# Gate steps, merge loads and the final norm moved in a one-core encoder layer

## The chip, the cores and the metric

The kernel runs on one core of a Trainium2 chip. The metric is the device time of one execution in microseconds (us); the figure for a kernel is the median of its runs. TensorE (PE, with its weight loads PEld) multiplies; VectorE (DVE), ScalarE (ACT) and GpSimd (POOL) do the element-wise work; SyncE (SP) issues the transfers. Each engine runs its instructions in the order in which they are queued.

## The reference, cut to what matters

One layer of a streaming encoder works on 1024 prompt frames and 64 sample frames (T = 1088 columns) of width 1024, in float32.

```
h = x + 0.5 * SwiGLU_1(RMSNorm(x))
u = RMSNorm(h);  z = u @ W_in        -> q, k, v, q_idx, k_idx, w_idx, conv_in, gate
attn = top-k attention: per query the 256 best admissible keys by indexer score
       (48 for the sample frames), softmax over them, 8 heads on 2 key/value heads
conv = swish(LayerNorm(causal depthwise conv of GLU(conv_in))) @ conv_w_out
merged = sigmoid(g_a) * (attn @ attn_w_out) + sigmoid(g_c) * conv
h = h + merged @ W_out
h = h + 0.5 * SwiGLU_2(RMSNorm(h))
y = RMSNorm(h) * final_norm
```

The new keys, values, indexer keys and last convolution inputs are outputs too.

## The kernel before, in words

Activations lie transposed, channels on the 128 partitions and frames along the free axis. Every float32 product is made of three TensorE products (`mm3`, lines 134 to 138): weights and activations are split into a high part and a remainder, and high*high, high*low and low*high are added up in PSUM. So each operand is split first: ACT copies out the high part (L152 for activations, L118 and L326 for weights) and DVE or POOL subtracts (L153, L119, L327). The two SwiGLU stages use a 7-product scheme on 2x2 blocks of weights and halves of 272 frames (`wops`, `up`, `down`).

The stages follow each other: load x and take the sums of squares (`stats`, with `colsum` on TensorE, a Newton iteration on DVE in `rsqrt`, and `spread`, which puts the result on all partitions through TensorE and `ident`); SwiGLU 1 for two pairs of halves; the projections of u; indexer and top-k selection, while TensorE makes the first 12 of the 16 gate matrices (`GPRE`); attention; W_out; SwiGLU 2; final norm. Before the first SwiGLU, `prep` makes the split operands of the scheme out of the first half (POOL does half of the remainders) and then out of the second half.

**The attention stage** (L1172 to L1471) handles nine tiles of 128 queries (the last has 64) in the order 7, 6, 8, 5, 4, 3, 2, 1, 0, four pairs of heads each: 36 units. `soft` makes the logits in PSUM banks of the pool `lg` (3 banks; L1209, L1210), DVE adds the bias and takes the maximum (L1212), ACT takes the exponential and scales. `turn` transposes the shares on TensorE (`pt`, L1233) and splits them; `values` multiplies with the values (`pv`, one bank; L1253, L1254), and `oh` is stored to `d_at` (L1260, L1261). After each of the 84 slots `fill` (L1453) advances other work by a rate out of `RATE`, so that TensorE has something to do beside the softmax: `gate_part` (the last gate matrices, three steps of 24 products each, and the LayerNorm of chunk 2), `conv_part` (the convolution's output product for the three chunks of `CHUNKS`, with the other two LayerNorms; it reads gates `gc` and stores `d_mp`), `merge_part` (chunk 2: attention output product, both gates, split), `wout_part` (chunk 2 of W_out, added to h in DRAM) and `last_part` (merge of chunk 1). `merge` for a chunk may only begin when all tiles of the chunk are done (`ready`); its first step loads four pieces `ar` of `d_at` and splits them into `ah` and `al`. What is left, and chunk 1 and 0 of W_out, runs behind the attention.

The order on each engine is not the order of the program text: the tile framework schedules the instructions by priority (`high_priority`) and by its own estimate of when operands are there. Tiles of a pool are handed out in rotation, and a new tile waits until the old one in its place has been read.

**The end**: `tail_d` runs the sums of squares of the last two halves behind the last down products; `final` spreads the result and makes eight scalings on DVE (`scaled`, L211) of h by gain and by the spread row, each stored to y.

## Time and profile before

| | us |
|---|---|
| three runs | 2315.79, 2320.89, 2318.33 |
| median | 2318.33 |
| the profiled execution | 2322.28 |
| its span, first to last instruction | 2320.5 |
| TensorE busy in the span | 2244.1 |
| mean granted TensorE clock | 0.988 of full |

The span is 1.8 us shorter than the time of its execution. In the views below, a row of the timeline has start, duration, engine, line, operation, result and operands, shape, count, and in brackets the idle time of the engine ahead of it with what ended it. A row of waits has the sum, the number of times and the longest. A row of the chain has start, duration and what.

### The profile page before, as it was taken

To read this page: it belongs to the slowest core of one execution; us is meant where nothing else is said; L and a number is where in the kernel's file an instruction comes from. 1 tells how busy PE (TensorE), PEld (TensorE's weight loads), DVE (VectorE), ACT (ScalarE), POOL (GpSimd) and SP (SyncE) were. 2 spreads that over 40 slices of the span, in tenths; PEclk is the share of its full clock that TensorE was granted. 3 is DMA by queue.
4 is the path that set the end of the run, shared out by engine and by line. 5 is a ranking of instruction groups with operands and counts; after the bars stand their busy time and mean duration, and the time that the engine had idled before them with its cause. 6 is when DMAs were issued, how large, how long until landed. Compare 5 with 4: busy or idle time off the path is not lost. (4 is left out here: it accounts for less than half of the span.)

```text
span 2320.5 us, 44122 instructions
## 1 busy us (share of the span) xinstructions
PE 2244.1 (97%) x16226; PEld 2213.2 (95%) x16226; DVE 1672.9 (72%) x3816; ACT 1415.6 (61%) x2955; POOL 1440.0 (62%) x1003
## 2 busy tenths in 40 slices
PE   7999999999999999999989989899999999999997
PEld 6999999999999999999989989799999999999997
DVE  7887766777676378689956766567877667887765
ACT  7655555666546454797457877557665556555653
POOL 5677655677766593788711333367667666667754
PEclk9999999999999999999999999899999999999999
DMA  5322233233223434334422566652222332322323
GB/s 190 109 103 99 101 101 104 100 100 110 101 92 126 146 127 134 95 111 123 134 64 86 161 192 198 220 173 101 97 102 94 110 110 73 111 101 101 105 97 112
DMA packets 129547, 273.39 MB, mean 118 GB/s; under 512 B 17840, under 2 KB 77104, under 8 KB 129328
## 3 DMA queue, kind: packets, MB, share of 16 engines
q1 hardware_dynamic: 129328, 270.56, 35.1%
q8 instruction: 127, 2.08, 0.4%
q14 instruction: 92, 0.75, 0.1%
HBM read 231.82 MB, written 38.75 MB: 117 GB/s over the span
## 5 line engine op out<-in xcount | busy, mean ns | idle before, releaser
L136 PE MATMUL ps<-x,wp 128*128 128x272 f32 x1760 | 507.1, 289 | 6.2 <-ACT wp L152 3.3
L138 PE MATMUL ps<-x,wp 128*128 128x272 f32 x1760 | 503.7, 291 | 3.5 <-DVE wp L153 2.0
L137 PE MATMUL ps<-x,wp 128*128 128x272 f32 x1760 | 505.8, 288 | 0.0
L136 PE MATMUL ps<-x,whi 128*128 128x272 f32 (+2 forms) x1544 | 481.8, 312 | 6.4 <-ACT x L152 2.2
L153 POOL TENSOR_TENSOR wp<-s,wp 128x512 fp32r<-128x512 f32 x272 | 364.6, 1352 | 190.7 <-ACT wp L152 189.9
L138 PE MATMUL ps<-x,wlo 128*128 128x272 f32 (+2 forms) x1544 | 481.1, 312 | 0.0
L119 POOL TENSOR_TENSOR wlo<-raw,whi 128x1024 fp32r<-128x1024 f32 (+1 forms) x123 | 279.1, 2270 | 298.2 <-ACT whi L118 293.3
L137 PE MATMUL ps<-x,whi 128*128 128x272 f32 (+2 forms) x1334 | 412.1, 309 | 1.0 <-POOL x L153 1.0
L327 POOL TENSOR_TENSOR wlo<-raw,whi 128x1024 fp32r<-128x1024 f32 x120 | 290.1, 2418 | 179.5 <-ACT whi L326 161.5
L136 PEld LDWEIGHTS ps<-x,wp 128*128 128x128 f32 x1760 | 330.7, 188 | 9.9 <-ACT wp L152 4.8
L138 PEld LDWEIGHTS ps<-x,wp 128*128 128x128 f32 x1760 | 328.0, 188 | 6.9 <-DVE wp L153 3.8
L137 PEld LDWEIGHTS ps<-x,wp 128*128 128x128 f32 x1760 | 331.3, 188 | 0.0
L136 PEld LDWEIGHTS ps<-x,whi 128*128 128x128 f32 x1544 | 292.8, 190 | 8.7 <-ACT x L152 2.6
L138 PEld LDWEIGHTS ps<-x,wlo 128*128 128x128 f32 x1544 | 292.7, 190 | 1.0
L137 PEld LDWEIGHTS ps<-x,whi 128*128 128x128 f32 x1334 | 253.5, 190 | 2.5 <-POOL x L153 1.3
L152 ACT ACTIVATE wp<-s 128x512 fp32r<-128x512 f32 x272 | 167.9, 626 | 130.9 <-DVE s L314 83.6
L784 POOL TENSOR_TENSOR ac<-ac,pd 128x559 f32<-128x559 f32 (+1 forms) x132 | 194.8, 1476 | 23.0 <-ACT pd L783 15.5
L152 ACT ACTIVATE wp<-ps 128x512 fp32r<-128x512 f32 x208 | 123.1, 592 | 113.1 <-DVE ps L312 103.3
L439 DVE SCALAR_TENSOR_TENSOR h<-ps,h 128x272 f32<-128x272 f32 x448 | 175.0, 430 | 14.0 <-PE ps L138 12.7
L137 PE MATMUL ps<-gl,whi 128*128 128x272 f32 x640 | 183.4, 292 | 0.0
L137 PE MATMUL ps<-gl,wp 128*128 128x272 f32 x640 | 181.0, 288 | 0.0
L136 PE MATMUL ps<-gh,wp 128*128 128x272 f32 x640 | 179.0, 290 | 1.9 <-DVE h L439 1.8
(288 smaller groups left out, 5784.4 us busy)
## 6 DMA issues: line engine op xcount, KB each, us to landing
raw<-wf SPq DMA_DIRECT2D x353, 512.0 KB, 3.3
d_g<-sg SPq DMA_DIRECT2D x32, 181.0 KB, 1.9
d_h<-h SPq DMA_DIRECT2D x2, 2176.0 KB, 10.0
y<-t SPq DMA_DIRECT2D x32, 136.0 KB, 1.9
raw<-wf SPq DMA_DIRECT2D x16, 256.0 KB, 2.7
raw<-d_q SPq DMA_DIRECT2D x32, 128.0 KB, 3.7
raw<-d_qi SPq DMA_DIRECT2D x24, 128.0 KB, 3.1
d_g<-sg SPq DMA_DIRECT2D x16, 182.0 KB, 3.2
```

Of the source, the lines that this page charges most:

```text
L119: self.weng.tensor_tensor(lo[:, :n], raw[:, :n], hi[:, :n], op=ALU.subtract)
L136: t.matmul(out, wh, xh, start=first, stop=False, skip_group_check=onto)
L137: t.matmul(out, wh, xl, start=False, stop=False, skip_group_check=onto)
L138: t.matmul(out, wl, xh, start=False, stop=last, skip_group_check=onto)
L152: nc.scalar.activation(hi, x, AF.Copy)
L153: (eng or nc.vector).tensor_tensor(lo, x, hi, op=ALU.subtract)
L327: self.weng.tensor_tensor(lo, raw, hi, op=ALU.subtract)
L439: nc.vector.scalar_tensor_tensor(x, p, 0.5, x, op0=ALU.mult, op1=ALU.add)
L784: nc.gpsimd.tensor_tensor(ac, ac, pd, op=ALU.add)
```

## The change

- Start: x's first half is loaded ahead of `par` and `ident`, these ahead of its second half, and all of it ahead of weights; before, `par` and `ident` came behind the second half and three weights. `warm` makes products whose results nobody reads: 26 on `ones`, and 7 behind each of the first two column sums. The two `hb` activations stand later in the program.
- Attention: two gate steps (`FIRST`) are issued ahead of the first logits; the PSUM pools are opened in the order `psa`, `pv`, `lg`, `psf` instead of `lg`, `psf`, `psa`, `pv`; the rates change; `begin` loads and splits the pieces of a merge as soon as its tiles are done (chunk 2 once the last convolution chunk runs, chunk 1 from the W_out part on), with four load buffers and in the tiles that held the split convolution; one step of W_out for chunk 2 (`HOLD`) is held back until after the merge of chunk 1; for tiles 1 and 0 every second pair takes its value bank from `lg`.
- End: for the half of the third final norm, POOL makes five of the eight scalings, in two steps each, and DVE three; for the last half, ACT multiplies h by the gain as each block is finished, and behind the spread five blocks are multiplied on DVE and three on POOL, from a copy in SBUF that ACT makes. Eight `warm` products follow the last column sum.

```diff
-RATE = (0.5, 1.0, 1.0, 0.5, 1.0)
+FIRST = 2
+HOLD = 1
+RATE = (0.42, 0.9, 1.0, 0.44, 1.0, 1.0)
...
+    def warm(self, x, n):
+        ps = self.psum()
+        for _ in range(n):
+            self.nc.tensor.matmul(ps[:, 0:P], x, self.ones, start=True, stop=True)
...
-            res.append(self.rsqrt(self.colsum([acc], w), 1.0 / D, tmp))
+            c = self.colsum([acc], w)
+            if warm:
+                self.warm(acc[:, 0:P], warm)
+            res.append(self.rsqrt(c, 1.0 / D, tmp))
...
+    def gained(self, x, h, k, t0, w, par):
+        q = PAR[par][0] + k
+        self.nc.scalar.activation(x, h[:, k, t0:t0 + w], AF.Copy, scale=self.par[:, q:q + 1])
...
-                with tc.high_priority(2 * WAHEAD - t0):
+                with tc.high_priority((4 if t0 == 0 else 2) * WAHEAD):
                     for k in range(0, KT, 2):
                         nc.sync.dma_start(h[:, k:k + 2, t0:t0 + HW], x_[:, k:k + 2, t0:t0 + HW])
+                if t0 == 0:
+                    with tc.high_priority(3 * WAHEAD):
+                        nc.sync.dma_start(self.par, a["par"])
+                        nc.sync.dma_start(ident, a["ident"])
...
+            self.warm(self.ones, 26)
...
-            ss = [self.stats(h, t0, HW, tp, ys[t0 // (2 * HW)]) for t0 in range(0, T, HW)]
+            ss = [self.stats(h, t0, HW, tp, ys[t0 // (2 * HW)], 7 if t0 < 2 * HW else 0) for t0 in range(0, T, HW)]
...
+            psa = self.pool(at_es, "psa", NPT, space=PS)
+            pvp = self.pool(at_es, "pv", 1, space=PS)
             lgp = self.pool(at_es, "lg", NLG, space=PS)
             psf = self.pool(at_es, "psf", 7 - NLG - NPT, space=PS)
-            psa = self.pool(at_es, "psa", NPT, space=PS)
-            pvp = self.pool(at_es, "pv", 1, space=PS)
...
-                    u.pv = pvp.tile([P, 512], F32, name="pv", tag="pv")[:, 0:n]
+                    pool, bank = (lgp, "lg") if u.i < 2 and u.h0 % 4 else (pvp, "pv")
+                    u.pv = pool.tile([P, 512], F32, name=bank, tag=bank)[:, 0:n]
...
+            def begin(c):
+                c0, w = CHUNKS[c]
+                lq = C["lq"]
+                A[c] = ah, al = [lq.tile([P, 4, WMAX], F32R, name=n, tag=t)[:, :, :w]
+                                 for n, t in (("ah", "ch"), ("al", "cl"))]
+                for k in range(4):
+                    ar = lq.tile([P, WMAX], F32, name="ar", tag="ar", bufs=4)[:, :w]
+                    nc.sync.dma_start(ar, d_at[k * P:(k + 1) * P, c0:c0 + w])
+                    self.split(ah[:, k, :], al[:, k, :], ar, nc.gpsimd if k % 2 else nc.vector)
...
             def wout_part():
-                yield from wout(2, h_dram(self.mp))
+                C["wout"] = wout(2, h_dram(self.mp))
+                yield from islice(C["wout"], 8 - HOLD)
...
+            def rest_part():
+                yield from C["wout"]
...
             def fill(units, n):
+                if C.get("from") and 2 not in A and ready(2):
+                    begin(2)
+                if state[0] > 2 and 1 not in A and ready(1):
+                    begin(1)
                 state[1] += RATE[state[0]]
...
+            steps = gates(gorder[GPRE:], ak, 2)
+            for _ in range(FIRST):
+                next(steps)
             attention(units, fill)
...
+            def final2():
+                r, rs = spread_final(2)
+                for k in range(KT):
+                    x = tp.tile([P, HW], F32, name="t", tag="t")
+                    if k % 3:
+                        nc.gpsimd.tensor_tensor(x, h[:, k, 0:HW], rs, op=ALU.mult)
+                        nc.gpsimd.tensor_scalar(x, x, par("final", k), None, op0=ALU.mult)
+                    else:
+                        self.scaled(x, h, k, 0, HW, "final", r)
...
-            run(final(3))
+            r, rs = spread_final(3)
+            for k, x in enumerate(ready):
+                if k % 3 == 1:
+                    nc.gpsimd.tensor_tensor(x, x, rs, op=ALU.mult)
+                else:
+                    nc.vector.tensor_tensor(x, x, r, op=ALU.mult)
+                nc.sync.dma_start(y_[:, k, HW:2 * HW], x)
```

How the change orders the engines is shown at three places. First TensorE at the start of the program, before the change; `ones` and `acc` are the operands of the column sums, `ident` and `ry` those of the spread, `x` and `whi`/`wlo` those of the first SwiGLU products:

```order
L166 MATMUL ps<-ones,acc 128x128 x6
L175 MATMUL ps<-ident,ry 128x128 x2
L175 MATMUL ps<-ident,ry 128x16
L136 MATMUL ps<-x,whi 128x272 x2
L137 MATMUL ps<-x,whi 128x272
L138 MATMUL ps<-x,wlo 128x272
```

And the same place in the changed kernel:

```order
L199 MATMUL ps<-ones 128x128 x26
L168 MATMUL ps<-ones,acc 128x128 x3
L199 MATMUL ps<-ones,acc 128x128 x7
L168 MATMUL ps<-ones,acc 128x128 x3
L199 MATMUL ps<-ones,acc 128x128 x7
L177 MATMUL ps<-ident,ry 128x128 x2
L177 MATMUL ps<-ident,ry 128x16
L138 MATMUL ps<-x,whi 128x272 x2
L177 MATMUL ps<-ident,ry 128x128 x2
L177 MATMUL ps<-ident,ry 128x16
L139 MATMUL ps<-x,whi 128x272
L140 MATMUL ps<-x,wlo 128x272
```

The small products stand around the column sums, and the second spread, which came behind the first twelve SwiGLU products, now stands ahead of the first product with a remainder (L139, before L137).

Second, TensorE at the start of the attention stage, before the change; `lg` are logits, and the products with `x` or `u` and `whi`/`wlo` are gate steps, 364 columns wide for chunk 0 and 362 for the others:

```order
L138 MATMUL ps<-x,wlo 128x362
L1209 MATMUL lg<-kh_13801,qt 128x512
L1210 MATMUL lg<-kl_13802,qt 128x512
L1209 MATMUL lg<-kh_13801,qt 128x512
L1210 MATMUL lg<-kl_13802,qt 128x512
L1209 MATMUL lg<-kh_13801,qt 128x512
L1210 MATMUL lg<-kl_13802,qt 128x512
L136 MATMUL ps<-x,whi 128x364
```

The same place now:

```order
L140 MATMUL ps<-x,wlo 128x362
L1226 MATMUL lg<-kh_13844,qt 128x512
L1227 MATMUL lg<-kl_13845,qt 128x512
L1226 MATMUL lg<-kh_13844,qt 128x512
L1227 MATMUL lg<-kl_13845,qt 128x512
L1226 MATMUL lg<-kh_13844,qt 128x512
L1227 MATMUL lg<-kl_13845,qt 128x512
L138 MATMUL ps<-x,whi 128x362
```

Before, the logits were followed by the first step of a gate matrix (364 wide); now they are followed by its third (362 wide), 19 products of which stand ahead of the fourth pair of logits: the first two steps, 48 products, stand ahead of the logits.

Third, SP's queue where the pieces for the merge of chunk 2 are loaded, before the change; `d_at<-oh` stores a finished unit, 17 of which stand ahead of the first load; `gc` and `d_mp` belong to the convolution's output, `ga` and `mpt` to the merge:

```order
L1261 DMA d_at<-oh 64x2x128
L1361 DMA ar<-d_at 128x362
L1345 DMA d_mp<-gc 128x364
L1361 DMA ar<-d_at 128x362
L1368 DMA ga<-d_g 128x362
L1370 DMA mpt<-d_mp 128x362
```

The same place now:

```order
L1279 DMA d_at<-oh 64x2x128
L1379 DMA ar<-d_at 128x362
L119 DMA raw<-wf 128x1024
L1279 DMA d_at<-oh 64x2x128
L1363 DMA d_mp<-gc 128x362
L1379 DMA ar<-d_at 128x362
L1361 DMA gc<-d_g 128x362
```

The first load stood behind 17 stores of units; now it stands behind the 13th, directly behind the store that it needs, and the other three behind the 14th, 15th and 16th, with weights, gate loads and convolution stores behind them.

## The prediction

> **What bounds the kernel now.** The profile page comes first.

> ```profile
> span 2320.5 us, 44122 instructions
> PE 2244.1 (97%) x16226; PEld 2213.2 (95%) x16226; DVE 1672.9 (72%) x3816; ACT 1415.6 (61%) x2955; POOL 1440.0 (62%) x1003
> ```

> TensorE is busy for 2244.1 of 2320.5 us, so a change that takes no products away can win only what TensorE idles (76 us) and what it works at a lower clock. The table of windows says where; its columns are stretch, length, busy time of PE, PEld, DVE, ACT and POOL, the granted clock, the DMA share, GB/s.

> ```profile
> 27.50:30.90 3.40, 1.65 (x14) 1.43 (x12) 2.77 (x8) 3.37 (x8) 2.49 (x2) 1.00 0.01 2
> 30.90:34.30 3.40, 3.40 (x18) 3.40 (x17) 2.94 (x8) 3.40 (x11) 2.92 (x3) 0.50 0.46 159
> 1171.00:1498.70 327.70, 302.83 (x1930) 290.37 (x1928) 207.72 (x551) 238.96 (x507) 99.72 (x50) 0.95 0.48 150
> 1184.60:1191.50 6.90, 6.06 (x18) 5.50 (x19) 4.28 (x13) 3.86 (x6) 0.00 (x0) 0.51 0.00 0
> 1386.00:1392.80 6.80, 5.61 (x21) 5.22 (x22) 5.45 (x14) 6.72 (x16) 3.02 (x2) 0.50 0.06 16
> 1461.10:1464.50 3.40, 3.40 (x13) 2.86 (x14) 1.62 (x9) 3.37 (x13) 0.00 (x0) 0.50 0.12 35
> 1467.90:1471.30 3.40, 3.40 (x14) 3.15 (x14) 1.62 (x5) 3.09 (x13) 0.39 (x1) 0.50 0.07 19
> 1485.00:1488.40 3.40, 1.06 (x7) 0.85 (x6) 2.80 (x6) 1.74 (x4) 1.00 (x2) 1.00 0.79 271
> 1488.40:1498.70 10.30, 6.86 (x22) 6.27 (x22) 3.27 (x5) 1.75 (x4) 1.84 (x1) 0.50 0.93 307
> ```

> The attention stage, 1171 to 1498.7, holds 327.70 - 302.83 = 24.9 us of idle. A wait costs twice: a stretch with little work (1.65 of 3.40 us before 30.9) is followed by one at clock 0.50, in which the products take twice as long. So the stage also loses half of the busy time in the slow stretches shown: 3.0, 2.8, 1.7, 1.7 and 3.4 us. DVE and ACT are busy for 63% and 73% of it, so neither is the bound. Who is waited for there, from the view of waits:

> ```profile
> PE lg L1209 <- DVE mb L1212: 7.5, 5, 4.4
> PE ps L136 <- ACT ah L152: 5.0, 3, 2.3
> PE pv L1253 <- DVE oh L1260: 4.9, 3, 2.7
> PE lg L1209 <- ACT sg L1162: 1.8, 1, 1.8
> PE ps L136 <- DVE oh L1260: 1.6, 1, 1.6
> ```

> Logits wait for DVE, the merge for the split of its loads, the values for their one bank. Each has an edit of its own.

> **Gate steps ahead of the logits.** The timeline at the start of the stage:

> ```profile
> 1175.27 0.50 PE L1209 MATMUL lg<-kh,qt 128*128 128x512 f32 x1 [1.76 <-ACT sg L1162]
> 1176.76 0.33 PE L136 MATMUL ps<-x,whi 128*128 128x364 f32 x1
> 1180.76 0.33 PE L136 MATMUL ps<-x,whi 128*128 128x362 f32 x1
> 1184.69 0.69 DVE L1212 CUSTOM_DVE_ANT_0 pr<-lg,bias 128x512 f32<-128x512 f32 x1 [3.01 <-issue]
> 1185.44 0.80 PE L1209 MATMUL lg<-kh,qt 128*128 128x512 f32 x1 [4.35 <-DVE mb L1212]
> ```

> TensorE waits 1.76 us for a bank of the old pool, then 4.35 us because DVE reaches its first softmax step only at 1184.69. One gate step (24 products, 1176.76 to 1180.76) takes 4.00 us. In the changed order two stand ahead: from 1175.27 - 1.76 = 1173.5 they last to 1181.5; three pairs of logits (1176.76 - 1175.27 = 1.5) to 1183.0; then 19 products of the next step, by 4.00/24 each, to 1186.2. That is after 1185.44, when the first of the three logits banks was free again. The new order of the PSUM pools puts these steps into banks of the indexer, idle by then. So 1.76 + 4.35 + 3.0 of slow clock: **9.1 us less**. The cover is DVE's time; had DVE come 5 us later, that much would stay.

> **Merge loads.** Between 1372 and 1393:

> ```profile
> 1373.37 0.50 PE L1209 MATMUL lg<-kh,qt 128*128 128x512 f32 x1 [2.44 <-DVE mb L1212]
> 1387.19 0.97 PE L136 MATMUL ps<-ah,whi 128*128 128x362 f32 x2 [2.02 <-ACT ah L152]
> ```

> ```profile
> ACT ah L152 <- DMA ar<-d_at: 6.2, 4, 2.8
> ```

> ```profile
> ar<-d_at SPq DMA_DIRECT2D x8, 181.0 KB, 3.6
> d_at<-oh SPq DMA_DIRECT2D x19, 64.0 KB, 2.3
> ```

> The wait for ah should go: its loads now stand some twenty rows of the SP queue earlier, among the last convolution output. The 2.44 us can stay. The place holds 2.44 + 2.02 + 2.8 = 7.3 us; I take **4.5 less**. But now each of the four loads of chunk 2 stands directly behind the store it needs: SP waits for the store (2.3 us to landing, the median), the split on ACT for the load (3.6), and behind these wait SP's gate loads and weights, ACT's softmax steps, DVE's softmax and value splits, and TensorE for them. That is up to 5.9 us for each. Four waits of ACT for such loads were 6.2 us together, and not all reached TensorE: I charge **4 more**, with 0 and 23.6 as ends.

> **Shares, second bank, held step.** At the end TensorE idles 3.40 - 1.06 = 2.3 and 10.30 - 6.86 = 3.4 us, and half of 6.86 goes to the slow clock: 9.2 us. Now alternate pairs of the last two tiles use a logits bank, and one held output step of 4 us stands between the merge and the steps that need it: **7.5 less**. What the stage has besides is 24.9 - 6.1 - 4.5 - 5.8 = 8.5 idle and 3.4 of clock, spread over short waits. A thinner filler leaves those of chunk 1's loads, whose stores they still follow directly: 3.5 of 11.9, **3.5 less**. The held step's store to d_h goes onto SP with a load of h and weights behind it; up to three raw and three split weights ahead hide that, else a step of 4 us waits.

> **The start.**

> ```profile
> 12.42 6.98 POOL L327 TENSOR_TENSOR wlo<-raw,whi 128x1024 fp32r<-128x1024 f32 x3 [11.47 <-ACT whi L326]
> 20.17 0.59 PE L137 MATMUL ps<-x,whi 128*128 128x272 f32 x1 [0.98 <-POOL x L153]
> 20.79 0.43 PE L136 MATMUL ps<-x,whi 128*128 128x272 f32 x1
> 24.23 0.51 DVE L211 SCALAR_TENSOR_TENSOR ps<-h,par,ps 128x272 f32<-128x272 f32 x1 [3.34 <-ACT gf L347]
> 24.36 0.29 PE L136 MATMUL ps<-x,whi 128*128 128x272 f32 x1
> 30.43 0.39 PE L136 MATMUL ps<-x,whi 128*128 128x272 f32 x1 [1.75 <-ACT gf L347]
> ```

> POOL's three splits set 20.17; they start with the first weights, which par and ident now push back by an estimated 0.5 us (160 KB at the 307 KB/us of the last window above). DVE then stood 3.34 us because the second spread came only after TensorE's first product; it now stands ahead of it, so DVE's preparation, and with it the end of the 1.75 us wait, comes some 3 us earlier. If less idle keeps the clock, 1.7 us at 30.9 go too. I take **4 less**, between 1.5 and 5.5. The products on ones fill time before the first sums; a late end of the 26 would cost up to 1 us. The two hb activations now stand on ACT behind the first sum's squares, whose successors wait if par lands late; par lands early in the queue, so I price them at nothing.

> The stretch ahead of 30.9 was half busy, and was still followed by clock 0.50. [...]

> **The end.**

> ```profile
> 2301.22 0.84 PE L175 MATMUL ps<-ident,ry 128*128 128x128 f32 x6 [0.47 <-DVE ry L191]
> ```

> ```profile
> 2306.41 0.29 PE L138 MATMUL ps<-gh,wlo 128*128 128x272 f32 x1
> ```

> ```profile
> 2307.64 0.36 DVE h L515
> 2312.08 1.47 PE ps L175 x6
> 2313.58 2.35 DVE t L211 x6
> 2316.47 0.50 DVE t L211
> ```

> ```profile
> L153 POOL TENSOR_TENSOR x<-t,x 128x272 fp32r<-128x272 f32 x28 | 21.4, 774 | 26.6 <-ACT x L152 26.4
> ```

> The last product ends at 2306.70, DVE adds it at 2307.64: 0.9 us late behind eight scalings, of which five go to POOL. The spread takes 1.47 us, and 0.84 at full clock, which the eight products after the sum should keep: 0.6. Then eight multiplies (2313.58 to 2316.97, 3.4 us) become five on DVE (2.1) beside a copy on ACT (0.4) and three on POOL (2.3, all behind the copy): 0.6. **2 less**, between 3 less and 1 more if POOL's per-channel scalings, which no row shows, take twice a row's 774 ns. The eight scalings by gain on ACT come before the spread is there and delay nothing; were ACT behind, its copy would be late by one of them (0.4).

> **How the numbers follow.** -4 - 9.1 - 4.5 + 4 - 7.5 - 3.5 - 2 = -26.6. The profiled execution took 2322.3 us with its launch, 4.0 above the median of the three runs, so it would become 2295.7 and the median 2318.3 become **2292**. Measurements here tell 0.2%, 4.6 us, from no change.

> - Forecast, 0.48: as summed, 2284 to 2300.
> - The merge's waits only move, 0.2: nothing at the merge or in the short waits, 4 for the loads: 2318.3 - 4 - 9.1 + 4 - 7.5 - 2 = 2300. The 2.44 us behind DVE speak for it; that ah's own 5.0 us have a cover now, against.
> - Slower, 0.09: the four loads of chunk 2 each hold ACT and DVE for the whole 5.9 us, TensorE runs dry, and a slow stretch (1.7) follows each: 30.4 in place of the net 4 gained there and in the short waits, 2326. It decides from about 5.7 us a load, slow stretch included (the 22.6 gained elsewhere, over 4). For it: TensorE waited on ah in three of the old places. Against: longest wait 2.8.
> - POOL pays for its first scaling by a scalar, 0.08. Its first kind of instruction started right behind ACT at 12.42, after 11.47 us of idle in which a set-up of any length up to that could hide. In the last 18 us it would lie bare: ten steps of 774 ns from 2302.5 (the spread at 2302.06 and its copy) end at 2310.2, before the last spread; 11.5 later they end at 2321.7 and the three multiplies at 2324.0 instead of about 2314.9: up to 9 more, 2301. [...]
> - All waits of the stage close, 0.15: 9.1 + 7.3 + 9.2 + 11.9 = 37.5, and 6 at the ends: 2275.

> The range 2278 to 2308 leaves out the slower case and half of the last. Faster by over 0.2%: all but the third, 0.91. Of the third, 0.03 fall within 0.2%, 0.06 beyond.

> **What would show it.** Right: no TensorE idle over 1 us between the last gate step and the first transposes; the end of attention without waits on oh and at clock 1.00; the second spread ahead of the first full product and no slow stretch near 30; the last spread in 0.84 us. Wrong: waits of ACT on ar over 3 us each with TensorE waiting on lg or pt behind them; SP's gate loads late; POOL idle ahead of its first scaling; the stage longer than 310 us from its first logits to its last value.

## The result, and the profile after

Six runs of the changed kernel took 2292.86 to 2303.30 us, with a median of 2298.07, beside 2318.10 for six runs of the kernel before. The ratio is 0.9921, with a 95% interval from 0.9905 to 0.9936: faster by 18 us (15 to 22). The prediction said 2292, in a range from 2278 to 2308. Of all the runs below one, of e3_old_merge_loads, took 9634.73 us; it is in no ratio, and its cause is not known. The profiled execution of the changed kernel took 2297.45 us. The head of its page:

```profile
span 2295.6 us, 44327 instructions
PE 2241.7 (98%) x16322; PEld 2212.5 (96%) x16322; DVE 1676.0 (73%) x3808; ACT 1416.0 (62%) x2965; POOL 1450.3 (63%) x1016
```

TensorE worked 2.4 us less, small products included, and the span is 24.9 us shorter: what went is for the most part idle time. To see where, the same three products are looked up in both timelines: a spread within the first SwiGLU, the first logits of the indexer, a spread within the second SwiGLU. First the kernel before:

```profile
372.20 0.38 PE L175 MATMUL ps<-ident,ry 128*128 128x128 f32 x1 [1.46 <-DVE h L515]
902.07 0.50 PE L943 MATMUL lgi<-khi,qt 128*128 128x512 f32 x1 [0.66 <-DVE qt L802]
1916.67 0.38 PE L175 MATMUL ps<-ident,ry 128*128 128x128 f32 x1 [1.45 <-DVE h L515]
```

The changed kernel:

```profile
369.57 0.38 PE L177 MATMUL ps<-ident,ry 128*128 128x128 f32 x1 [1.46 <-DVE h L529]
898.07 0.51 PE L960 MATMUL lgi<-khi,qt 128*128 128x512 f32 x1 [0.90 <-DVE qt L819]
1891.89 0.38 PE L177 MATMUL ps<-ident,ry 128*128 128x128 f32 x1 [1.45 <-DVE h L529]
```

| part of the program | before, us | changed, us | difference |
|---|---|---|---|
| start to the first spread | 372.20 | 369.57 | -2.6 |
| to the indexer | 529.87 | 528.50 | -1.4 |
| indexer, attention, W_out, to the second spread | 1014.60 | 993.82 | -20.8 |
| to the end of the span | 403.83 | 403.75 | -0.1 |

The 1.4 us need not be the change's: the stretch at half clock that follows 792 in the kernel before is not there in this execution, and is there again, at 790.6, in e8 below, whose engines run the same instructions in the same order. The third line holds the attention stage. The windows of the kernel before; columns as in the prediction:

```profile
1171.00:1200.00 29.00, 22.88 (x119) 20.89 (x118) 16.19 (x38) 13.40 (x21) 2.38 (x1) 0.88 0.13 45
1340.00:1400.00 60.00, 53.99 (x336) 50.79 (x335) 38.27 (x95) 46.69 (x96) 21.95 (x12) 0.94 0.66 199
1440.00:1510.00 70.00, 59.61 (x343) 56.82 (x343) 36.24 (x100) 41.81 (x111) 24.38 (x12) 0.88 0.66 218
1171.00:1510.00 339.00, 314.13 (x1998) 301.67 (x1997) 210.55 (x557) 244.29 (x517) 105.42 (x53) 0.95 0.50 157
```

And of the changed kernel:

```profile
1171.00:1200.00 29.00, 29.00 (x176) 27.66 (x175) 16.44 (x40) 17.56 (x29) 4.37 (x2) 1.00 0.20 70
1340.00:1400.00 60.00, 53.68 (x336) 50.86 (x336) 42.56 (x96) 45.74 (x97) 20.11 (x9) 0.97 0.70 214
1440.00:1510.00 70.00, 64.35 (x386) 63.18 (x385) 35.47 (x87) 34.66 (x75) 37.54 (x18) 0.98 0.72 246
1171.00:1510.00 339.00, 324.64 (x2127) 314.03 (x2126) 223.56 (x585) 252.94 (x533) 121.74 (x61) 0.99 0.53 169
```

At the first logits nothing is idle any more. Around the merge of chunk 2 the idle time stayed (6.0 us and 6.3). At the end of the stage it fell from 10.4 us to 5.7, and the clock there rose from 0.88 to 0.98. TensorE's waits in the changed stage have other names than before:

```profile
PE pt L1250 <- DVE pl L155: 6.4, 5, 3.4
PE ps L138 <- DVE hr L1410: 2.6, 1, 2.6
PE ps L140 <- POOL wlo L121: 1.8, 1, 1.8
PE ps L138 <- DVE gc L1362: 1.6, 1, 1.6
```

The longest, 3.4 us, can be followed in the timelines of SP, DVE and TensorE:

```profile
1363.34 0.39 SPq L1392 DMA_DIRECT2D ga<-d_g  x1
1369.80 0.54 DVE L1397 SCALAR_TENSOR_TENSOR ps<-ga,ps 128x362 f32<-128x362 f32 x1 [3.68 <-DMA ga<-d_g]
1370.25 0.42 DVE L155 TENSOR_TENSOR pl<-pt,ph 128x256 fp32r<-128x256 f32 x1
1370.81 0.45 PE L1250 MATMUL pt<-ident,pr 128*128 128x128 f32 x1 [3.37 <-DVE pl L155]
```

The first gate of the merge is asked for at 1363.34, behind weights and queries, and DVE gets it at 1369.80. In DVE's queue the split of the shares stands behind that, and TensorE's next transposes behind the split.

At the end of the program the spread and POOL's scalings came about as computed, the stores did not. The timelines of POOL, TensorE, ACT, DVE and SP:

```profile
2278.83 2.99 POOL L1571 TENSOR_TENSOR t<-h,rs 128x272 f32<-128x272 f32 x4 [3.68 <-ACT rs L1563]
2281.86 2.88 POOL L1572 TENSOR_SCALAR t<-t,par 128x272 f32<-128x272 f32 x3
2287.40 0.84 PE L177 MATMUL ps<-ident,ry 128*128 128x128 f32 x6 [0.41 <-DVE ry L193]
2288.36 0.40 ACT L1563 ACTIVATE rs<-ps 128x272 f32<-128x272 f32 x1 [4.18 <-PE ps L177]
2288.79 1.83 DVE L1601 TENSOR_TENSOR f<-f,ps 128x272 f32<-128x272 f32 x5 [1.44 <-ACT rs L1563]
2289.26 3.77 SPq L1602 DMA_DIRECT2D y<-f  x8
```

The spread takes 0.84 us instead of 1.47, and POOL's scalings by a scalar take 0.96 us each, without a pause. But SP needs 3.77 us for eight stores, 0.47 each, whereas DVE and POOL need 2.25 us for the eight multiplications (2288.79 to 2291.04). From the spread's end to the span's end it was 7.0 us before (2320.5 - 2313.55) and is 7.4 now (2295.6 - 2288.24).

### The profile page after: what moved, and what is told of

It is laid out like the page before. It is cut to its first block, busy times and chain, and to the rows that moved or that the text cites. A ratio compares the mean times of both kernels' runs of the same rounds, so it can differ in the third digit from the quotient of the medians.

```text
span 2295.6 us, 44327 instructions
## 1 busy us (share of the span) xinstructions
PE 2241.7 (98%) x16322; PEld 2212.5 (96%) x16322; DVE 1676.0 (73%) x3808; ACT 1416.0 (62%) x2965; POOL 1450.3 (63%) x1016
## 5 line engine op out<-in xcount | busy, mean ns | idle before, releaser
L138 PE MATMUL ps<-x,wp 128*128 128x272 f32 x1760 | 506.9, 289 | 4.5 <-ACT wp L154 1.9
L139 PE MATMUL ps<-x,wp 128*128 128x272 f32 x1760 | 505.8, 288 | 0.0
L138 PE MATMUL ps<-x,whi 128*128 128x272 f32 (+2 forms) x1544 | 479.8, 311 | 4.8 <-ACT x L154 2.4
L139 PE MATMUL ps<-x,whi 128*128 128x272 f32 (+2 forms) x1334 | 410.3, 308 | 0.0
L138 PEld LDWEIGHTS ps<-x,wp 128*128 128x128 f32 x1760 | 330.6, 188 | 8.2 <-ACT wp L154 4.0
L139 PEld LDWEIGHTS ps<-x,wp 128*128 128x128 f32 x1760 | 331.4, 188 | 0.0
L138 PEld LDWEIGHTS ps<-x,whi 128*128 128x128 f32 x1544 | 291.3, 189 | 6.6 <-ACT x L154 2.7
L139 PEld LDWEIGHTS ps<-x,whi 128*128 128x128 f32 x1334 | 252.1, 189 | 1.1
L139 PE MATMUL ps<-gl,whi 128*128 128x272 f32 x640 | 183.3, 292 | 0.0
L138 PE MATMUL ps<-gh,whi 128*128 128x272 f32 x640 | 175.9, 292 | 6.5 <-DVE spare L298 3.9
L138 PE MATMUL ps<-gh,wp 128*128 128x272 f32 x640 | 179.0, 290 | 2.2 <-DVE h L453 2.1
## 6 DMA issues: line engine op xcount, KB each, us to landing
d_g<-sg SPq DMA_DIRECT2D x32, 181.0 KB, 1.9
```

The lines of the kernel that those rows point to most:

```text
L138: t.matmul(out, wh, xh, start=first, stop=False, skip_group_check=onto)
L139: t.matmul(out, wh, xl, start=False, stop=False, skip_group_check=onto)
```

## The experiments

Each experiment changes the changed kernel, but for one that changes the kernel before. The ratio is to the kernel before on the same chip.

| experiment | median, us | before, us | ratio | 95% interval |
|---|---|---|---|---|
| changed kernel, as above | 2298.07 | 2318.10 | 0.9921 | 0.9905 to 0.9936 |
| e0_no_calls | 2306.33 | 2321.47 | 0.9935 | 0.9921 to 0.9949 |
| e1_no_warm_start | 2308.41 | 2321.47 | 0.9947 | 0.9932 to 0.9963 |
| e2_no_first | 2303.00 | 2321.47 | 0.9923 | 0.9909 to 0.9937 |
| e3_old_merge_loads | 2315.27 | 2321.47 | 0.9972 | 0.9960 to 0.9984 |
| e4_old_pools | 2306.49 | 2319.71 | 0.9941 | 0.9928 to 0.9954 |
| e5_one_bank | 2304.37 | 2319.71 | 0.9933 | 0.9914 to 0.9951 |
| e6_no_hold | 2311.06 | 2319.71 | 0.9959 | 0.9946 to 0.9972 |
| e7_early_gates_two_queues | 2304.95 | 2319.71 | 0.9932 | 0.9919 to 0.9945 |
| e8_again | 2305.76 | 2320.67 | 0.9936 | 0.9917 to 0.9955 |
| e9_old_with_gate_steps | 2319.49 | 2320.67 | 0.9988 | 0.9975 to 1.0000 |
| e10_old_rates | 2315.95 | 2320.67 | 0.9978 | 0.9967 to 0.9988 |
| e11_hold_two | 2310.17 | 2320.67 | 0.9951 | 0.9936 to 0.9965 |

e0 and e8 are the changed kernel but for two calls that are left out, and serve as its measure on their chips: 0.9935 and 0.9936. Two such ratios are told apart when they differ by about 0.002 or more, that is by 4.6 us. By that only e3 (8.6 us slower), e10 (9.7) and e6 (5.6) differ from the changed kernel, e6 just so: e4 to e7 ran on a third chip, where the changed kernel itself was not run, and e6's interval overlaps those of e0 and e8.

### The same instructions twice more: e0 and e8

```diff
             def fill(units, n):
-                if C.get("from") and 2 not in A and ready(2):
-                    begin(2)
-                if state[0] > 2 and 1 not in A and ready(1):
-                    begin(1)
```

> The changed kernel with the two calls of begin in fill left out; merge calls begin itself. Theory (it is not the call but the four load buffers and the slots of the split convolution that let the loads go early, since every engine's order stays the same): the same time, 2298 within 3 us, with the same waits: about 3.4 us of TensorE behind pl near 1371, 1.6 behind gc near 1350, 2.5 near 1467. Rival (the early calls are what brings the merge's loads forward): slower by the 4.5 us that the prediction took for the loads, 2302.5.

> The changed kernel with the two calls of begin in fill left out, as in the first experiment, once more on the chip of the next three. Theory (the same instructions meet the same waits, and the time differs by how many waits end in a stretch at half clock, each worth 1.7 us): the waits near the places 1270, 1350, 1371, 1467 and 1491 of the changed kernel's profile again within 0.5 us, and 2296 to 2306 in all. Rival (chips differ in the waits themselves): one of these waits gone or doubled.

Every engine's instructions come out in the same order without the calls: the scheduler moves the loads forward by itself, once their buffers allow it. So both are repeats of the changed kernel, and yet they took 2306.33 and 2305.76 us. In the attention stage the sums of e0's waits are the same to 0.3 us, row by row. What differs there is what follows a wait. A stretch of the changed kernel that ends with its wait for gc, and the stretch behind it:

```profile
1346.90:1350.30 3.40, 1.82 (x10) 1.26 (x9) 0.61 (x4) 2.48 (x4) 1.30 (x1) 1.00 0.52 158
1350.30:1353.70 3.40, 3.36 (x22) 3.23 (x23) 1.77 (x5) 0.00 (x0) 1.06 (x1) 1.00 0.91 288
```

The same two in e0:

```profile
1352.60:1356.00 3.40, 1.82 (x10) 1.24 (x9) 0.82 (x3) 2.25 (x4) 1.54 (x1) 0.99 0.65 150
1356.00:1359.40 3.40, 3.40 (x14) 3.31 (x14) 1.50 (x5) 0.00 (x0) 0.82 (x1) 0.51 0.86 282
```

With 1.82 us of work in 3.40, one execution keeps the full clock and the other falls to half. Between 40 and 2290 us the changed kernel's execution spent 13.7 us at half clock, that of e0 23.9, that of e8 27.3, that of the kernel before 44.4. Half of the difference between the first two, 5.1 us, is over half of the 9.0 us between their spans (2295.6 and 2304.6); another 2.0 are a wait ahead of the indexer, 2.88 us in e0 and 0.90 in the changed kernel. In e8 the wait near 1371 was 5.1 us in place of 3.4, a 2.5 us wait for weights stood near 1497, and the wait for gc was gone: the theory that the waits repeat within 0.5 us held for e0 only, and e8 itself went as its rival said.

### The gate steps and the pools: e2, e4 and e9

```diff
-FIRST = 2
+FIRST = 0
```

> The changed kernel with no gate steps ahead of the first logits (FIRST = 0); the new order of the PSUM pools stays. Theory (the two steps fill the time until DVE reaches its first softmax step): an idle stretch of about 4.4 us of TensorE returns behind the first three pairs of logits, with a slow stretch of 3 us of loss behind it; the wait of 1.8 us ahead of the first logits stays away, since its bank comes from the pool order; 7.3 us slower, about 2305. Rival (the order of the pools does it all): no idle stretch over 1 us there, 2298 within 3.

```diff
-            psa = self.pool(at_es, "psa", NPT, space=PS)
-            pvp = self.pool(at_es, "pv", 1, space=PS)
             lgp = self.pool(at_es, "lg", NLG, space=PS)
             psf = self.pool(at_es, "psf", 7 - NLG - NPT, space=PS)
+            psa = self.pool(at_es, "psa", NPT, space=PS)
+            pvp = self.pool(at_es, "pv", 1, space=PS)
```

> The changed kernel with the PSUM pools of the attention stage opened in the old order; TensorE's order stays the same. Theory (the order of the pools is what took the waits around the first logits away, since without the two gate steps ahead only 1.5 us stood idle there): TensorE waits again for the bank of an old gate step, 1.8 us or more around the first logits, 2 to 5 us slower, 2300 to 2303 where the changed kernel takes 2298. Rival (either of the two edits is enough by itself): no idle stretch over 1 us there, the same time within 2 us.

TensorE's wait at the first logits in e2, and the wait around them in e4:

```profile
1185.22 0.50 PE L1226 MATMUL lg<-kh,qt 128*128 128x512 f32 x1 [1.47 <-DVE mb L1229]
```

```profile
1172.80 0.43 PE L138 MATMUL ps<-x,whi 128*128 128x364 f32 x1 [1.48 <-ACT sg L1179]
```

Each edit alone leaves 1.5 us of the 6.1 idle, and neither undoing changes the time by what can be told (0.9923 and 0.9941). So either edit is enough for most of that place, though not for all of it as the rivals said; in e2 the scheduler put 29 more products ahead of the logits than before, without being told. e9 asks the other question, what both edits are worth in the kernel before. Its edit there, beside the new order of the pools:

```diff
+FIRST = 2
...
-                steps = gates(gorder[GPRE:], ak, 2)
-                for _ in range(3 * (16 - GPRE) - 11):
+                for _ in range(3 * (16 - GPRE) - 11 - FIRST):
...
+            steps = gates(gorder[GPRE:], ak, 2)
+            for _ in range(FIRST):
+                next(steps)
             attention(units, fill)
```

> The kernel before with only the two gate steps ahead of the logits and the new order of the PSUM pools; rates, merge loads, value bank and both ends as before. Theory (the term of the sum stands by itself): no idle stretch over 1 us at the first logits, 9 us faster than before, 2309. Rival (the two steps are missing as filler later in the stage): the idle time of the stage falls by less than 3 us, since the waits at the merge and at the end grow, and the time by under 4 us.

```profile
1171.00:1200.00 29.00, 29.00 (x176) 27.79 (x175) 16.57 (x38) 14.24 (x23) 4.80 (x2) 1.00 0.22 74
1171.00:1510.00 339.00, 318.16 (x2048) 303.87 (x2047) 218.92 (x561) 247.86 (x524) 112.16 (x56) 0.97 0.52 161
```

```profile
PE pv L1254 <- DVE oh L1261: 5.2, 3, 4.2
1298.96 0.45 PE L1210 MATMUL lg<-kh,qt 128*128 128x384 f32 x1 [1.58 <-DVE mb L1213]
1303.85 0.58 PE L167 MATMUL ps<-ones,ls 128*128 128x128 f32 x1 [2.12 <-POOL ls L1297]
```

The place is full, as predicted. But the medians differ by 0.12% (0 to 0.25%), 2.8 us in place of the 9 that the theory asked for, so the time is the rival's. In the profiled execution the stage's idle time falls from 24.9 us to 20.8, more than the rival's 3 us: later waits grew, mostly between 1200 and 1340 (2.4 us idle before, 5.6 now; the two rows shown), and by 0.5 us from 1440 to 1510. But this execution is not a typical one. Four of the eleven runs of e9 took 2311 to 2315 us and seven 2319 to 2322; the profile is of one of the four, 2313.54, and there the part from the indexer to the second spread is 8.4 us shorter than in the profile of the kernel before (902.99 to 1909.17). Where the seven lose what this one gains, no trace shows; that steps spent early are missing later fits the two rows, and is not shown for the median.

### The rates: e10

```diff
-RATE = (0.42, 0.9, 1.0, 0.44, 1.0, 1.0)
+RATE = (0.5, 1.0, 1.0, 0.5, 1.0, 1.0)
```

> The changed kernel with the old rates of the filler (0.5, 1.0, 1.0, 0.5, 1.0, and 1.0 for the rest). Theory (the thinner filler is part of the gain, since steps that run out early leave the last pairs uncovered): 3 to 6 us slower, with waits of TensorE in the last 40 us of the stage. Rival (the prediction's small price for the rates): the same time within 2 us to 3.5 us slower.

9.7 us slower, more than either side expected. The waits for ah are back, a long one for ga is new, and near 1300 stand the same two waits as in e9, 1.57 us at 1299.88 and the row shown, with 6.8 us at half clock from 1302.28. No profiled execution with the new rates waits longer than 0.7 us between 1290 and 1325:

```profile
PE ps L138 <- DVE ga L1398: 7.5, 2, 6.8
PE ps L138 <- ACT ah L154: 6.4, 5, 2.5
1304.52 0.58 PE L168 MATMUL ps<-ones,ls 128*128 128x128 f32 x1 [2.58 <-POOL ls L1314]
```

The first product of the merge of chunk 2 and the last of the four loads that it needs, in e10:

```profile
1362.38 0.33 PE L138 MATMUL ps<-ah,whi 128*128 128x362 f32 x1
1374.97 0.32 SPq L1379 DMA_DIRECT2D ar<-d_at  x1
```

And in the changed kernel:

```profile
1350.58 0.32 SPq L1379 DMA_DIRECT2D ar<-d_at  x1
1361.01 0.33 PE L138 MATMUL ps<-ah,whi 128*128 128x362 f32 x1
```

The load goes out 10.4 us ahead of the products with the new rates, and 12.6 us behind the first of them with the old. Counted from the stage's first logits (1177.31 and, in e10, 1183.17), the merge starts after 183.7 us with the new rates and after 179.2 with the old, and the attention has not come as far: of 152 value products 102 lie ahead of the first merge product in the changed kernel, 92 in e10, and 92 also in e9, which has the gate steps in front and the old rates. In the kernel before, with neither, it is 102. So the steps in front bring the filler forward, and the thinner rates hold it back to where the loads have their lead. The early buffers alone do not give it (e10), nor do the rates alone (e3 below).

### The merge's loads and the held step: e3, e6 and e11

```diff
-                if c not in A:
-                    begin(c)
-                ah, al = A[c]
+                ah = mp_.tile([P, 4, WMAX], F32R, name="ah", tag="ah")[:, :, :w]
+                al = mp_.tile([P, 4, WMAX], F32R, name="al", tag="al")[:, :, :w]
+                for k in range(4):
+                    ar = mp_.tile([P, WMAX], F32, name="ar", tag="ar", bufs=2)[:, :w]
+                    nc.sync.dma_start(ar, d_at[k * P:(k + 1) * P, c0:c0 + w])
+                    self.split(ah[:, k, :], al[:, k, :], ar, nc.gpsimd if k % 2 else nc.vector)
+                yield
...
-                    lq = C["lq"] = self.pool(ac_es, "lnq", 1, side="right")
+                    lq = C["lq"] = self.pool(cx, "lnq", 1, side="right")
```

The calls of `begin` in `fill` are left out too.

> The changed kernel with the merge's loads as before: two load buffers and own tiles for the split, allocated by the merge's first step. Theory (early loads take away the waits of the first merge products for ah): TensorE waits for ah again ahead of the first merge products, 2 to 5 us of idle in all with a slow stretch, while the waits for gc near 1350 and for pl near 1371 shrink, since SP no longer holds loads of attention output ahead of the gate loads; 2 to 5 us slower, 2300 to 2303. Rival (the waits only moved from the attention output to the gates, so nothing was won): 2298 within 2.

```diff
-HOLD = 1
+HOLD = 0
```

> The changed kernel with no output step held back (HOLD = 0). Theory (the held step fills 4 us that nothing else fills between the merge of chunk 1 and its output steps, less the wait of 2.5 us for DVE ahead of it): 2 to 4 us slower, with TensorE waiting for ga or xl there. Rival (the held step only moves the wait, since the transfers of the gates end late either way): the same time within 2 us.

8.6 us and 5.6 us slower. The wait for ah is there in e3 as expected (3.96 us at 1372.08), but the larger wait comes in the merge of chunk 1. SP's queue there, and TensorE:

```profile
1463.68 1.30 SPq L1512 DMA_DIRECT2D h<-d_h  x2
1465.08 4.24 SPq L1396 DMA_DIRECT2D ga<-d_g  x1
1478.40 0.67 PE L138 MATMUL ps<-ah,whi 128*128 128x362 f32 x1 [8.02 <-DVE ga L1402]
```

Two loads of h, of 1.4 MB each, stand ahead of a gate that the merge still needs. In e6 TensorE waits twice for ga behind such loads (issued at 1462.88, 1467.97 and 1472.15):

```profile
1473.39 0.67 PE L138 MATMUL ps<-ah,whi 128*128 128x362 f32 x1 [5.04 <-DVE ga L1398]
1482.11 0.64 PE L138 MATMUL ps<-xh,whi 128*128 128x362 f32 x1 [4.95 <-DVE ga L1398]
```

In e10 the loads of h go out at 1472.94, and 6.8 us of waiting for ga follow. In the changed kernel the merge is through when they start:

```profile
1459.63 0.32 PE L140 MATMUL ps<-ah,wlo 128*128 128x362 f32 x1
1460.42 1.29 SPq L1512 DMA_DIRECT2D h<-d_h  x2
```

By these traces the held step works less as four us of filler than by starting the merge of chunk 1 one step earlier, ahead of the loads of h. e2 does not fit well: there h is asked for at 1461.4, the merge lasts to 1467.6, and TensorE waits 4.9 us for ga at 1472.47, but the time is no longer. Holding two did not help:

```diff
-HOLD = 1
+HOLD = 2
```

> The changed kernel with two output steps held back in place of one. Theory (filler is what is short between the merge of chunk 1 and its output steps, where TensorE waits 2.5 us and 1.8 us): 2 to 4 us faster than the changed kernel, with both waits under 1 us. Rival (the waits are for gates and weights that land late, and a second held step only takes the place of one that covered another wait before): the same time within 2 us.

The wait for hr fell to 0.7 us, but there were 4.9 us for ga, 3.6 for weights and 2.4 for wlo, and the ratio is 0.9951. The theory of missing filler finds no support. That the loads of h are the cause was not tested by moving them.

### The value bank: e5

```diff
-                    pool, bank = (lgp, "lg") if u.i < 2 and u.h0 % 4 else (pvp, "pv")
+                    pool, bank = (pvp, "pv")
```

> The changed kernel with one bank for the values of all pairs. Theory (the second bank took away the waits for oh at the end of the attention, as predicted): two or three waits of TensorE for oh return between the last 40 us of the attention, 3 to 6 us of idle and a slow stretch or two of 1.7 us, 4 to 9 us slower. Rival (the held step and the merge of chunk 1 now stand between the last pairs and cover that): waits for oh under 1 us, the same time within 2 us.

The waits for oh come back as 2.4 and 0.9 us, as the theory said, but the time stays (0.9933), as the rival did. With the bank alternated, a wait for hr of 2.6 us stands at that place.

### The small products at the start: e1

```diff
-            self.warm(self.ones, 26)
...
-            ss = [self.stats(h, t0, HW, tp, ys[t0 // (2 * HW)], 7 if t0 < 2 * HW else 0) for t0 in range(0, T, HW)]
+            ss = [self.stats(h, t0, HW, tp, ys[t0 // (2 * HW)], 0) for t0 in range(0, T, HW)]
```

> The changed kernel without the 26 products ahead of the first column sum and the 7 behind each of the first two; the order of the loads stays. Theory (the gain at the start comes from the order of the transfers and of the second spread; the small products only move the full clock to 5.5 to 19.1 us, where little runs, and a slow stretch from 19.1 to 26.0 follows): TensorE at half clock until about 24 and then at full clock, the spread in front of the second SwiGLU part at 369.6 within 1.5 us, total 2298 within 3. Rival (the small products hold the clock for the first SwiGLU products): that spread 2 to 3 us later, total 2300 to 2301.

The spread within the first SwiGLU comes at 374.32, in e0 at 370.25:

```profile
123.92 0.39 PE L138 MATMUL ps<-x,wp 128*128 128x272 f32 x1 [1.71 <-ACT wp L154]
374.32 0.38 PE L177 MATMUL ps<-ident,ry 128*128 128x128 f32 x1 [1.46 <-DVE h L529]
```

That is 4.1 us later, and the theory is wrong in its 1.5. But by the hundredth product, at 36, the small products have brought only 0.9 us (36.8 in e1, 35.9 in e0). Most of the rest is this wait at 123.92, which the kernel before has too (1.91 us), and the half-clock stretch behind it (a mean clock of 0.91 from 112 to 130). ACT waits there for weights that land 4.55 us after their issue at 117.62; in e0 it is 3.22 us after 116.67. SP's transfers stand in the same order in both, so why this one took longer is open, and that the small products spare this wait is not shown. By the whole time (0.9947 beside 0.9935) the two are not told apart.

### Earlier gates and two queues for the stores: e7

```diff
-                    ga = mp_.tile([P, WMAX], F32, name="ga", tag="ga", bufs=3)[:, :w]
+                    ga = C["lq"].tile([P, WMAX], F32, name="ga", tag="gc", bufs=3)[:, :w]
...
-                    mpt = mp_.tile([P, WMAX], F32, name="mpt", tag="mpt", bufs=3)[:, :w]
+                    mpt = C["lq"].tile([P, WMAX], F32, name="mpt", tag="ar", bufs=4)[:, :w]
...
-                nc.sync.dma_start(y_[:, k, HW:2 * HW], x)
+                (nc.scalar if k % 2 else nc.sync).dma_start(y_[:, k, HW:2 * HW], x)
```

> The changed kernel with two edits. The gate loads ga of the merge and the loads mpt take buffers of the convolution's pool (tags gc and ar), so that they may go out before the convolution's last products; and four of the last eight stores are issued by ACT. Theory (the wait of 3.4 us near 1371 is for ga, whose load is issued only 0.1 us before its products begin and lands 6.3 us later; the last eight stores end late because SP issues one in 0.49 us): that wait under 1 us without the slow stretch behind it, 4 to 5 us less, and the last store issued 1.5 us earlier, together 5 to 7 us faster than the changed kernel. Rival (the transfer engines are full there, so that earlier gates only make other loads late): waits of the same sum elsewhere in 1340 to 1400, and only the 1.5 us of the end.

The rival held at the merge. The wait of 3.4 us is gone, but the idle time of the merge's stretch is what it was, 6.4 us in 60:

```profile
1340.00:1400.00 60.00, 53.55 (x318) 48.65 (x317) 40.62 (x92) 43.58 (x90) 21.27 (x10) 0.94 0.72 218
```

The end, from the last product to the end of the span, is 12.3 us in place of 12.9: the stores are issued within 2.4 us instead of 3.8, but the last one, of a block that POOL multiplies, can't go earlier, and 0.6 us remain of the 1.5. No version here beats the changed kernel by more than can be told.

## Why the prediction was right, and where it was not

**The total.** For the profiled execution the sum said -26.6; it is -24.8 (2322.28 to 2297.45). The other 4.6 us between 2291.7 (rounded to 2292) and 2298.07 are the step from that execution to the median: the profile of before lay 4.0 above its median, that of the changed kernel 0.6 below. The five terms of the stage come to -20.6, and the third line of the table to -20.8. That they come so near is in part luck, since single terms missed in both directions, as follows. On the chips of e0 and e8 the gain is 15 us. Of the difference between their profiled executions and that of the changed kernel, 9.0 and 9.6 us, half clock makes up 5.1 and 6.8.

**The start**, -4 between -1.5 and -5.5: -2.6 at the first spread. The second spread does stand ahead of the first full product, and no slow stretch follows near 30, as said. But of the 2.6 us only 1.1 are there by 82 us (the 400th SwiGLU product stands at 81.84, before at 82.92), less than the near end of the range; the rest is the wait of 1.91 us at 123.91 in the kernel before, which is 0.43 us now and stood in no term. And the small products did not keep the clock: TensorE does 0.92 us of work between 15.70 and 19.10, and runs at 0.51 from 19.10 to 26.00.

**Gate steps ahead of the logits**, -9.1: right at its place, where nothing is idle. The step that failed is that the place was priced by itself. In e9 the same two edits bring 2.8 us by the medians, and at most 5.8 by the interval. With the old rates the filler then runs ahead: two waits near 1300 cost 3.7 us in e9 and 4.2 in e10, where the kernel before has one of 1.7, and they are gone with the new rates. The prediction named a cover for DVE's time, and none for the steps taken from later. How the rest of the 9 us is lost is open.

**Merge loads**, -4.5 and +4 for new waits: at the merge of chunk 2 the idle time did not change (6.0 and 6.3 us), as the net of the two terms says, and it is the gates that are late, one of the signs listed as wrong. ACT's waits for ar are 4.5 us at the longest. The rival "the merge's waits only move" describes this place. But it is wrong of the whole: without the early loads 8.6 us are lost, mostly in the merge of chunk 1, behind the loads of h, which the prediction did not look at there.

**Second bank, held step**, -7.5: from 1440 to 1510, idle time and half of the busy time at half clock were 17.2 us before (10.4 + 6.8) and are 7.3 now (5.7 + 1.6). The size is near that of this term with the share of the short waits that lay there. The cause was not the one named: the bank shows no price that these runs can tell (e5), and the held step's 5.6 us go, by the traces of e6, with the place of the merge and not with cover. The clock at the end of the attention was not 1.00 throughout either: 3.4 us from 1466.38 ran at half.

**Short waits, by the rates**, -3.5: mis-sized. e10 shows 9.7 us for the rates. They decide how far the pairs are when the merge begins, which the prediction took for a matter of the queue alone, and they keep the waits near 1300 away.

**The end**, -2: -0.9. The late addition gave 0.76 (2.54 to 1.78 us from the last product's start to the column sum) and the spread 0.63, near the 0.9 and 0.6 of the sum. The multiplications gave nothing: SP's eight issues set the end, and DVE stands 0.43 us behind ACT's copy, for which it waits too. The pace of the stores stood in no term, though the trace of the kernel before shows it: its last eight stores go out from 2314.11 to 2317.88, 3.77 us as well.

**POOL's first scaling.** The rival's price isn't there: POOL's scaling begins at 2281.86, 0.04 us behind the step before it (2278.83 + 2.99). What stands for it on POOL's queue, from the view of its line:

```profile
L1572 POOLq MODIFY_POOL_CONFIG  x2: 38/38/38, 2281.7 to 2281.8; - x2
```

From the first change of configuration on the queue to that scaling it is 0.1 us.

## What to carry to other kernels

Filler work is a stock: what is spent at one wait shifts all that follows, so an edit to the order of a stage is priced over the whole stage. The parts of such a change need not add up: undoing three of them costs 8.6, 9.7 and 5.6 us, 24 together, where the whole change brings 15 on those chips. A wait names the last operand that was late, and taking it away shows the next one in the same queue (here ah, then the gates, then the loads of h); what decides is how far ahead of its use a load can go out, by its buffers and by how far the work that it waits for has come. For the end of a kernel, count the pace of issuing the stores (0.47 us each here), not only the arithmetic.

## What the runs showed of the hardware

At half clock a product of 272 columns starts 227 ns behind the one before it, at full clock 126 (medians, the same in both executions). That is 1.8 times as long and not twice, so a stretch of 3.41 us costs an estimated 1.5 us (3.41 less 126/227 of it), where 1.7 is counted above, and the 5.1 and 6.8 us of e0 and e8 become 4.5 and 6.0.

In the changed kernel all 779 transfers, which SP issues, landed in the order of their issue. A gate of 181 KB issued at 1363.34 behind queries and weights was there 6.3 us later, the longest of its kind between 1340 and 1400:

```profile
DMA to landing us min/median/max: 2.1/3.1/6.3
```
